# Newton steps of six mLSTM heads' normalization on GpSimd in place of VectorE

## The chip, the cores and the metric

The kernel runs on one NeuronCore of one Trainium2 chip. A core has a matrix engine (TensorE, PE in the profile, with PEld for its weight loads), a vector engine (VectorE, DVE), a scalar engine (ScalarE, ACT), GpSimd (POOL) and a queue that only issues DMAs (SyncE, SP). Each engine takes its own queue in order; semaphores order the engines against each other. The metric is the device time of one execution in microseconds (us).

## The reference

Two layers work on a sequence of 512 tokens of width 1024. The first is dilated window attention with a SwiGLU; the second, which the change touches, is an mLSTM mixer with eight heads and a SwiGLU. A final RMS norm follows. The end of the mLSTM mixer, cut to what matters:

```python
h = num / jnp.maximum(jnp.abs(den), jnp.exp(-m_t))[..., None]      # per head and token, 128 wide
...
h = h * lax.rsqrt(jnp.mean(h * h, axis=-1, keepdims=True) + RMS_EPS)
h = h.reshape(B, S, D_MODEL).astype(xn.dtype) * head_gain.astype(xn.dtype)
return (h * jax.nn.sigmoid(o_pre)) @ w_out
```

So each of the 8 heads needs one reciprocal square root per token: 512 numbers, which the kernel holds as 128 partitions by 4.

## The kernel before

All matrix products run on TensorE in a split form (a high and a low part of each operand, three products in place of one), 128 rows at a time, with 512 tokens as the free dimension. Weights come in chunks by SP's DMAs; ScalarE makes the high part of a chunk (line 209) and VectorE the low part (line 210, names ending in `_l`).

In the mLSTM stage the projections run as a stream of such products: `mqk` (queries and keys), `mv` (values, line 272), `mo` (output gate), then `mwo` (output product, line 240). The heads are threaded through that stream. For head h the function `decay` makes the exponent mask, `scores` the masked products (`m{h}s`, lines 1541 and 1542, weighted on VectorE in line 1543 into `m{h}e`), and `numerators` the rest: the numerators and denominators `m{h}num` on TensorE (line 1553), in two PSUM banks under the tag `o`, of which there are two; so the next head's numerators need the banks back. Then, on VectorE unless said otherwise:

- the denominators are copied to `rr` (line 1561), their absolute value and the lower bound taken (`aa`, 1562 and 1563), and inverted (1564);
- ScalarE squares the four blocks of the numerators, scaled by `rr`, and sums them into `s2` (line 1567); VectorE makes the mean and adds epsilon (1569);
- `rsqrt_newton` (lines 184 to 195) computes 1/sqrt of `s2`: an integer guess `y` in two operations (189, 190) and three Newton steps of three operations each (192, 193, 194), all on 128x4 elements;
- `rr` is multiplied by it (1571), and four operations scale the numerators out of PSUM into `yt` (1574), which frees the banks, the first with the second operation;
- for heads 0 to 5 a transpose in 32x32 blocks follows (`yB`, 1581), four DMAs to DRAM and one back (`yD`, `y`, lines 1584 and 1587), all issued by GpSimd. Heads 6 and 7 (`LAST_OUTPUTS`) are transposed on TensorE instead (`outputs`, `m6yT`, `m7yT`).

The result `y[h]` is multiplied by the gate later (line 1621). `rsqrt_newton` also serves the RMS norms (`inverse_rms`).

The program gives the work in one order, with `defer` and `at_tick` placing the heads' functions in the stream of projections. A planner of the language then writes each engine's queue, by its own estimate of when each instruction can start; so a change of one instruction's engine can move others on all queues. Beside its DMAs GpSimd copies `ql` (line 1512) and clears buffers in this stage. Near the kernel's end it scales the final gain (line 1659) and multiplies by it (1684).

Of the kernel before, what the change touches and what calls it, by code (L numbers as in the profile page):

```python
# [15 lines left out]
ALU = mybir.AluOpType  # L16
# [6 lines left out]
TB = SEQ // P  # L23
# [16 lines left out]
LAST_OUTPUTS = {6: 22, 7: 23}  # L40
# [31 lines left out]
def tile_hybrid_dilated_attn_mlstm(  # L72
# [4 lines left out]
    nc = tc.nc  # L77
# [3 lines left out]
    def pool(stack, name, **kw):  # L81
        return stack.enter_context(tc.tile_pool(name=name, bufs=1, **kw))
# [98 lines left out]
    def acc_tile(name):  # L181
        return ps.tile([P, 512], F32, tag="acc", name=name, bufs=3)

    def rsqrt_newton(tp_pool, v, n, name, y=None):

        if y is None:
            y = tp_pool.tile([P, n], F32, tag="rs_y%d" % n, name=name + "_y", bufs=2)
        a = tp_pool.tile([P, n], F32, tag="rs_a%d" % n, name=name + "_a", bufs=2)
        nc.vector.tensor_single_scalar(a.bitcast(I32), v.bitcast(I32), 1, op=ALU.arith_shift_right)
        nc.vector.tensor_scalar(y.bitcast(I32), a.bitcast(I32), -1, 0x5F3759DF, op0=ALU.mult, op1=ALU.add)  # L190
        for _ in range(3):
            nc.vector.scalar_tensor_tensor(a, y, -0.5, y, op0=ALU.mult, op1=ALU.mult)
            nc.vector.tensor_tensor(a, a, v, op=ALU.mult)
            nc.vector.scalar_tensor_tensor(y, a, 1.5, y, op0=ALU.add, op1=ALU.mult)
        return y
# [112 lines left out]
    def inverse_rms(v, name, box=None, then=None):  # L308
# [5 lines left out]
        def finish():  # L314
            nc.vector.tensor_scalar(v, v, 1.0 / D, EPS, op0=ALU.mult, op1=ALU.add)
            rsqrt_newton(npl, v, TB, name + "r", r)
            rhl = npl.tile([P, 2, TB], F32R, tag="rhl", name=name + "rhl", bufs=2)
            nc.vector.tensor_copy(rhl[:, 0], r)
            nc.vector.tensor_tensor(rhl[:, 1], r, rhl[:, 0].bitcast(F32), op=ALU.subtract)
            for part in range(2):  # L320
                dg = parts[part] = npl.tile([P, SEQ], F32R, tag=("ssum", "sq")[part], name=name + "dg",
                                               bufs=1 + part)
                for tb in range(TB):
                    nc.vector.tensor_scalar(dg[:, tb * P:(tb + 1) * P], ident,
                                            rhl[:, part, tb:tb + 1].bitcast(F32), None, op0=ALU.mult)
# [20 lines left out]
    with ExitStack() as actx:  # L346
# [16 lines left out]
        ang, n, sn, cs = (tmp[:, 0, i * P:(i + 1) * P] for i in range(4))  # L363
# [132 lines left out]
        v = npl.tile([P, TB], F32, tag="rs_v4", name="xv", bufs=2)  # L496
# [781 lines left out]
    with ExitStack() as fctx:  # L1278
# [34 lines left out]
        def copy_half(t):  # L1313
            for m in range(4):
                nc.scalar.activation(F[1][m][:, ts[t]], F[0][m][:, ts[t]], AF.Copy)

        def add_sum(n):
            for m in range(4):
                o = old[4 * n + m][:, ts[1]]
                nc.vector.tensor_tensor(o, F[1][m][:, ts[0]], o, op=ALU.add)  # L1320

        def first_tiles():
            for m in range(4):
                natural(m, F[0][m])
        last = work(product, plain, {("P1", 3): lambda: copy_half(0), ("P5", 3): lambda: copy_half(1),
                                     ("P6", 3): lambda: add_sum(0), ("P7", 3): lambda: add_sum(1),
                                     ("P3", 3): first_tiles})
# [8 lines left out]
    with ExitStack() as mctx:  # L1336
        mp = pool(mctx, "mlstm")
# [6 lines left out]
        def y_tile(k, name):  # L1344
            return mp.tile([P, SEQ], F32, tag="my%d" % k, name=name)
# [94 lines left out]
        for b in range(TB):  # L1440
            ve.scalar_tensor_tensor(fblk[32 * b:32 * b + H], blk(lf)[:, b], bias2[:, 1:2], blk(t0)[:, b],
                                    op0=ALU.add, op1=ALU.add)
# [72 lines left out]
        y = [None] * H  # L1515
# [29 lines left out]
        def numerators(hh):  # L1545
            nm = "m%d" % hh
            sm = sms[hh]
            num = [ps.tile([P, 512], F32, tag="o", name=nm + "num", bufs=2) for _ in range(2)]
            nv = lambda qb: num[qb // 2][:, (qb % 2) * 256:(qb % 2) * 256 + P + 1]
            for qb in range(TB):  # L1550
                for kb in range(qb + 1):
                    o = (qb - kb) * P
                    nc.tensor.matmul(nv(qb), sm[kb][:, o:o + P], vaug[:, kb, hh, :],
                                     start=(kb == 0), stop=(kb == qb))

            rr = mp.tile([P, TB], F32, tag="rr", name=nm + "rr", bufs=2)
            aa = mp.tile([P, TB], F32, tag="aa", name=nm + "aa", bufs=2)
            s2 = mp.tile([P, TB], F32, tag="s2", name=nm + "s2", bufs=2)
            for t in range(2):
                den = num[t].rearrange("p (a b) -> p a b", a=2)[:, :, P]  # L1560
                nc.vector.tensor_copy(rr[:, 2 * t:2 * t + 2], den)
            nc.vector.scalar_tensor_tensor(aa, rr, -1.0, rr, op0=ALU.mult, op1=ALU.max)
            nc.vector.tensor_tensor(aa, aa, bcol[:, npair:, hh], op=ALU.max)
            nc.vector.reciprocal(rr, aa)
            for qb in range(TB):
                junk = mp.tile([P, P], F32, tag="junk", name=nm + "j", bufs=2)
                nc.scalar.activation(junk, nv(qb)[:, :P], AF.Square, scale=rr[:, qb:qb + 1],
                                     accum_out=s2[:, qb:qb + 1])
            nc.vector.tensor_scalar(s2, s2, 1.0 / P, EPS, op0=ALU.mult, op1=ALU.add)
            rq = rsqrt_newton(mp, s2, TB, nm + "rq")  # L1570
            nc.vector.tensor_tensor(rr, rr, rq, op=ALU.mult)
            yt = mp.tile([P, SEQ], F32, tag="yt", name=nm + "yt", bufs=2)
            for qb in range(TB):
                nc.vector.tensor_scalar(yt[:, qb * P:(qb + 1) * P], nv(qb)[:, :P], rr[:, qb:qb + 1], None,
                                        op0=ALU.mult)
            if hh in LAST_OUTPUTS:
                yts[hh] = yt
                return

            turned = npl.tile([P, SEQ], F32, tag="sq", name=nm + "yB", bufs=2)  # L1580
            nc.vector.transpose(turned.rearrange("p (c i) -> p c i", i=R), yt.rearrange("p (c i) -> p c i", i=R))
            d = mdp.tile([P, SEQ], F32, tag="yD", name=nm + "yD", bufs=3)
            for a in range(TB):
                nc.gpsimd.dma_start(d.rearrange("(f j) (q a i) -> a j q f i", f=4, q=TB, a=4)[a],
                                    turned[R * a:R * (a + 1)].rearrange("p (q f i) -> p q f i", q=TB, f=4))
            y[hh] = y_tile(hh, "y%d" % hh)
            nc.gpsimd.dma_start(y[hh], d)

        def outputs(hh):
            tp = ps.tile([P, 512], F32, tag="t", name="m%dyT" % hh, bufs=1)  # L1590
            for qb in range(TB):
                transpose_into(tp, qb, yts[hh][:, qb * P:(qb + 1) * P])
            y[hh] = y_tile(hh, "y%d" % hh)
            nc.scalar.activation(y[hh], tp, AF.Copy)
# [6 lines left out]
        for hh, ts in enumerate(HEAD_AT):  # L1601
            for t, fn in zip(ts, (decay, scores, numerators)):
                at_tick(t, lambda hh=hh, fn=fn: fn(hh))
# [26 lines left out]
    with ExitStack() as fctx:  # L1630
# [60 lines left out]
        def copy_banks(to, src):  # L1691
            for m in range(2):
                nc.scalar.activation(to[m], src[m], AF.Copy)

        def add_banks(tbs, src):
            for m, tb in enumerate(tbs):
                nc.vector.tensor_tensor(ht[tb, 1], src[m], ht[tb, 1], op=ALU.add)
# [12 lines left out]
        def plain(n, pi, a, w):  # L1710
            for t in range(2):
                multiply_half(((c11, u_), (p5, c22))[n][t], a, t, w)

        last = work(product, plain, {("P1", 3): lambda: copy_banks(u_, c11), ("P5", 3): lambda: copy_banks(c22, p5),
                                     ("P6", 3): lambda: add_banks((0, 1), u_), ("P7", 3): lambda: add_banks((2, 3), u_),
                                     ("P4", 0): lambda: outputs((0, 1), p5), ("P4", 1): lambda: outputs((2, 3), c22)})
# [6 lines left out]
        for acc, tb, cs in tiles:  # L1723
# [10 lines left out]
            else:  # L1734

                v, r, a2 = fv[:, tb:tb + 1], fr[:, tb:tb + 1], fa[:, tb:tb + 1]
                nc.vector.scalar_tensor_tensor(v, fss[:, tb, 2:3], 1.0 / D, fpre[:, tb:tb + 1],
                                               op0=ALU.mult, op1=ALU.add)
# [33 lines left out]
```

## Time and profile before

| | us |
|---|---|
| median of three runs (1409.32 to 1410.51) | 1409.42 |
| the profiled execution | 1409.1 |
| its span in the profile | 1407.0 |
| TensorE busy in it | 1395.9 |
| VectorE busy | 1045.6 |
| ScalarE busy | 659.5 |
| GpSimd busy | 145.4 |

The profile page has six parts: busy times; the span in 40 slices; DMA queues; the chain of work that ended last; the costliest groups of instructions; DMA issues. Other views are asked of the trace: groups by tile or line (duration as least, median and greatest in ns, first and last start in us), who waited for whom (total us, times, longest), instructions in order of time (start, length, engine, line, operation, output and inputs, then the idle time ahead of it and what ended it), and busy time by windows. In a window's row stand the window, its length, then busy us and count of PE, PEld, DVE, ACT and POOL, then TensorE's granted clock, the DMA share and GB/s. The mLSTM stage's heads 0 to 7 lie between 920 and 1025 us. TensorE's busy time is modelled from pipelined instructions.

### The profile page before, as it was taken

The page shows a single profiled execution, that of the slowest core. Times are in us where ns is not written, and L with a number is a line of the kernel's source. Part 1 is how long each engine was busy: PE and PEld are TensorE (multiplying, and loading weights), DVE is VectorE, ACT ScalarE, POOL GpSimd, SP SyncE. Part 2 cuts the span into 40 slices and gives each one's busy share as a digit, 9 for nine tenths or more (in the row PEclk, how much of TensorE's full clock was granted, in tenths as well). Part 3 has the DMA queues.
Part 4 walks back from the last instruction along what each step waited for, and adds up shares of the span by engine and source line. Part 5 has one row for each costly group of instructions (what it writes and reads, how often), then busy time and mean ns, then how long its engine had stood idle before and what let it go on. Part 6 is the DMA issues. An engine that isn't in the chain of part 4 may idle for free.

```text
span 1407.0 us, 21031 instructions
## 1 busy us (share of the span) xinstructions
PE 1395.9 (99%) x8154; PEld 1235.5 (88%) x8154; DVE 1045.6 (74%) x1816; ACT 659.5 (47%) x1096; POOL 145.4 (10%) x216
## 2 busy tenths in 40 slices
PE   9999999999999999999999999999999999999998
PEld 7888888888888888999999998888888899999886
DVE  7866557566567298777877788998758888887785
ACT  5333224224225153444576354786534444458744
POOL 1011011002002000000010101113101230002111
PEclk9999999999999999999999999999999999999999
DMA  6346245334434444333264543234333553335871
GB/s 194 98 113 201 77 117 154 125 105 129 163 102 120 160 118 152 91 120 118 67 186 97 150 120 84 85 90 103 96 101 105 168 151 116 120 99 141 173 188 61
DMA packets 136381, 174.44 MB, mean 124 GB/s; under 512 B 8469, under 2 KB 111189, under 8 KB 136281
## 3 DMA queue, kind: packets, MB, share of 16 engines
q1 hardware_dynamic: 121088, 133.65, 30.3%
q0 software_dynamic: 13536, 38.33, 12.3%
q8 instruction: 64, 1.05, 0.3%
q10 hardware_dynamic: 1656, 1.12, 0.2%
q14 instruction: 37, 0.30, 0.1%
HBM read 157.34 MB, written 15.73 MB: 123 GB/s over the span
## 4 chain that ended last, share of the span: by engine, by line
PE 92%; DVE 5%; ACT 2%; issue 1%; ACTq 0%; DVEq 0%
PE fo L1292 8%; PE f0j_u L1017 5%; PE f1j_u L1017 5%; PE f1j L240 5%; PE f0j L240 5%; PE f1j_p L1017 3%; PE f0j_p L1017 3%; PE f1j_c L1017 3%; PE f0j_c L1017 3%; PE mwo L240 3%; PE awo L240 3%; PE mo L240 3%; PE finu L1674 2%; PE finc L1674 2%; PE finp L1674 2%; PE a3g12v L298 2%
## 5 line engine op out<-in xcount | busy, mean ns | idle before, releaser
L240 PE MATMUL f0j<-n_h,f0j_h 128*128 128x512 f32 x96 | 37.5, 390 | 0.0
L240 PE MATMUL f1j<-n_h,f1j_h 128*128 128x512 f32 x96 | 37.5, 390 | 0.0
L240 PE MATMUL f1j<-n_h,f1j_l 128*128 128x512 f32 x96 | 37.4, 389 | 0.0
L240 PE MATMUL f0j<-n_h,f0j_l 128*128 128x512 f32 x96 | 37.4, 389 | 0.0
L240 PE MATMUL f0j<-n_l,f0j_h 128*128 128x512 f32 x96 | 37.3, 389 | 0.0
L240 PE MATMUL f1j<-n_l,f1j_h 128*128 128x512 f32 x96 | 37.3, 389 | 0.0
L1135 POOL DMA_DIRECT2D f0S<-in_ffn_w_out_dram x7 | 6.5, 1019 | 265.6 <-ACT f0P L1114 146.6
L1644 POOL DMA_DIRECT2D hD<-hB x32 | 20.7, 653 | 96.3 <-DVE hB L1641 96.3
L539 DVE TENSOR_TENSOR rot<-rot,sinr 32x1024 f32<-32x1024 f32 x24 | 28.9, 1205 | 0.0
L240 PE MATMUL mo<-n_h,mo_k_h 128*128 128x512 f32 x64 | 25.3, 395 | 0.0
L240 PE MATMUL mo<-n_h,mo_k_l 128*128 128x512 f32 x64 | 25.2, 394 | 0.0
L240 PE MATMUL mo<-n_l,mo_k_h 128*128 128x512 f32 x64 | 25.1, 393 | 0.0
L240 PE MATMUL mqk<-n_h,mqk_k_h 128*128 128x512 f32 x64 | 25.1, 393 | 0.0
L240 PE MATMUL mwo<-yo_l,mwo_k_h 128*128 128x512 f32 x64 | 25.1, 393 | 0.0
L240 PE MATMUL mqk<-n_l,mqk_k_h 128*128 128x512 f32 x64 | 25.1, 392 | 0.0
L240 PE MATMUL awo<-ao_h,awo_k_h 128*128 128x512 f32 x64 | 25.1, 392 | 0.0
L240 PE MATMUL mwo<-yo_h,mwo_k_l 128*128 128x512 f32 x64 | 25.0, 391 | 0.0
L240 PE MATMUL mqk<-n_h,mqk_k_l 128*128 128x512 f32 x64 | 25.0, 390 | 0.0
L240 PE MATMUL awo<-ao_h,awo_k_l 128*128 128x512 f32 x64 | 25.0, 390 | 0.0
L240 PE MATMUL awo<-ao_l,awo_k_h 128*128 128x512 f32 x64 | 24.9, 390 | 0.0
L240 PE MATMUL mwo<-yo_h,mwo_k_h 128*128 128x512 f32 x64 | 24.9, 391 | 0.0
L240 PEld LDWEIGHTS f0j<-n_h,f0j_l 128*128 128x128 f32 x96 | 18.0, 188 | 3.8
(2271 smaller groups left out, 5427.9 us busy)
## 6 DMA issues: line engine op xcount, KB each, us to landing
f0j_w<-in_ffn_w_in_dram SPq DMA_DIRECT2D x28, 512.0 KB, 4.4
f1j_w<-in_ffn_w_in_dram SPq DMA_DIRECT2D x28, 512.0 KB, 4.1
f1T<-in_ffn_w_out_dram POOLq DMA_DIRECT2D x12, 512.0 KB, 7.0
awo_k_w<-in_attn_w_out_dram SPq DMA_DIRECT2D x8, 512.0 KB, 5.8
mv_k_w<-in_mlstm_w_in_dram SPq DMA_DIRECT2D x8, 512.0 KB, 3.7
mqk_k_w<-in_mlstm_w_in_dram SPq DMA_DIRECT2D x8, 512.0 KB, 3.8
mo_k_w<-in_mlstm_w_in_dram SPq DMA_DIRECT2D x8, 512.0 KB, 3.7
mwo_k_w<-in_mlstm_w_out_dram SPq DMA_DIRECT2D x8, 512.0 KB, 3.5
```

The costliest lines, as they stand in the source:

```text
L240: nc.tensor.matmul(acc, whl[a][:, k, m * P:(m + 1) * P], pairs[b][kk], start=(kk == 0 and (a, b) == SPLITS[0]), stop=(kk == nk - 1 and (a, ...
L298: nc.tensor.matmul(accs[tb], pairs[a][kk][:, tb * P:(tb + 1) * P], whl[b][:, k, :], start=(kk == 0 and (a, b) == SPLITS[0]), stop=(kk == K ...
L539: nc.vector.tensor_tensor(sh, sh, sinr.unsqueeze(1).to_broadcast([R, 2, SEQ]), op=ALU.mult)
L1017: nc.tensor.matmul(acc[name][:, m * HALF:(m + 1) * HALF], whl[a][:, k, m * P:(m + 1) * P], ops[okey][b][:, k], start=(fresh and m == 0 and ...
L1135: nc.gpsimd.dma_start(t, src[1][:, ks], accum_op=ALU.add)
L1292: nc.tensor.matmul(acc, w[a_][:, k, m * P:(m + 1) * P], b[b_][k], start=(fresh and k == 0 and (a_, b_) == SPLITS[0]), stop=(k == 1 and (a_ ...
L1644: nc.gpsimd.dma_start(hD[k // 4].rearrange("(b i) x -> i b x", i=R)[:, :, c0:c0 + R], t[R * a_:R * (a_ + 1)])
L1674: nc.tensor.matmul(acc[m], a[a_][k][:, (2 * t + m) * P:(2 * t + m + 1) * P], w[b_][:, k, :], start=(fresh and k == 0 and (a_, b_) == SPLIT ...
```

## The change

For heads 0 to 5 the three Newton steps and the product into `rr` are put on GpSimd. A step there has four operations in place of three, since the fused scalar-tensor-tensor form is written out as products and a scalar operation. The guess, the mean and the scaling stay on VectorE; heads 6 and 7 and the RMS norms stay as they were.

```diff
-    def rsqrt_newton(tp_pool, v, n, name, y=None):
+    def rsqrt_newton(tp_pool, v, n, name, y=None, on_gpsimd=False):
...
         for _ in range(3):
+            if on_gpsimd:
+                nc.gpsimd.tensor_tensor(a, y, y, op=ALU.mult)
+                nc.gpsimd.tensor_tensor(a, a, v, op=ALU.mult)
+                nc.gpsimd.tensor_scalar(a, a, -0.5, 1.5, op0=ALU.mult, op1=ALU.add)
+                nc.gpsimd.tensor_tensor(y, a, y, op=ALU.mult)
+                continue
             nc.vector.scalar_tensor_tensor(a, y, -0.5, y, op0=ALU.mult, op1=ALU.mult)
             nc.vector.tensor_tensor(a, a, v, op=ALU.mult)
             nc.vector.scalar_tensor_tensor(y, a, 1.5, y, op0=ALU.add, op1=ALU.mult)
...
-            rq = rsqrt_newton(mp, s2, TB, nm + "rq")
-            nc.vector.tensor_tensor(rr, rr, rq, op=ALU.mult)
+
+            last = hh in LAST_OUTPUTS
+            rq = rsqrt_newton(mp, s2, TB, nm + "rq", on_gpsimd=not last)
+            (nc.vector if last else nc.gpsimd).tensor_tensor(rr, rr, rq, op=ALU.mult)
```

In the built program the queues of TensorE, VectorE, ScalarE and GpSimd stand in another order between the first head and the last; SP's queue has the same order. On GpSimd a configuration step that stood ahead of line 1659 stands ahead of head 0's first Newton step.

## The prediction

> **What bounds the kernel now.** I read the page's busy shares first, then who waited for whom on TensorE, then the mLSTM stretch by windows and by tiles.
>
> ```profile
> span 1407.0 us, 21031 instructions
> PE 1395.9 (99%) x8154; PEld 1235.5 (88%) x8154; DVE 1045.6 (74%) x1816; ACT 659.5 (47%) x1096; POOL 145.4 (10%) x216
> ```
> ```profile
> PE m2num L1553 <- DVE m1yt L1574: 1.2, 1, 1.2
> ```
> ```profile
> 940.00:950.00 10.00, 10.00 (x85) 9.95 (x84) 9.66 (x27) 9.82 (x21) 1.40 (x3) 1.00 0.46 134
> 950.00:960.00 10.00, 8.76 (x59) 7.64 (x59) 8.67 (x27) 8.06 (x26) 3.56 (x5) 1.00 0.34 79
> ```
>
> TensorE (PE) is the bound: 1395.9 of 1407.0 us. In the stretch with the heads it loses 1.2 us to one wait, m2's numerators for m1's scaling (the window 950 to 960 shows the gap: 8.76 of 10). So the change can give back some 1.2 us, 0.1%. VectorE (DVE) is nearly full there (9.66 of 10), but PE does not wait for it. What the change can cost is decided by the chain of one head.
>
> ```profile
> L1553 PE MATMUL m0num<-vaug,m0e x20: 272/275/275, 921.6 to 923.7; 128*128 128x129 f32 x20
> L1553 PE MATMUL m1num<-vaug,m1e x20: 271/275/275, 933.9 to 936.1; 128*128 128x129 f32 x20
> L1553 PE MATMUL m2num<-vaug,m2e x20: 275/275/349, 952.0 to 954.2; 128*128 128x129 f32 x20
> L1553 PE MATMUL m3num<-vaug,m3e x20: 275/275/348, 963.6 to 965.8; 128*128 128x129 f32 x20
> L1553 PE MATMUL m4num<-vaug,m4e x20: 275/275/348, 975.1 to 977.3; 128*128 128x129 f32 x20
> L1553 PE MATMUL m5num<-vaug,m5e x20: 272/275/275, 986.9 to 989.0; 128*128 128x129 f32 x20
> L1553 PE MATMUL m6num<-vaug,m6e x20: 275/275/348, 997.3 to 999.5; 128*128 128x129 f32 x20
> ```
> ```profile
> L1574 DVE TENSOR_SCALAR m2yt<-m2num,m2rr x4: 343/343/352, 962.8 to 963.6; 128x128 f32<-128x128 f32 x4
> L1574 DVE TENSOR_SCALAR m4yt<-m4num,m4rr x4: 341/341/351, 986.1 to 986.9; 128x128 f32<-128x128 f32 x4
> ```
>
> Numerators of head h+1 need the first of the two PSUM banks that head h's scaling (yt) frees with its second operation. m2's yt begins at 962.8, its second operation ends some 0.7 us later, at 963.5, and m3num begins at 963.6; m4's yt begins at 986.1, and m5num at 986.9. PE stays busy until that moment because other matmuls are queued ahead of m3num in just that amount. PE takes its queue in order: whatever lengthens the way from num(h) to yt(h) beyond the matmuls queued between num(h) and num(h+1) stops PE. I call those matmuls the cover.
>
> **The change part by part.** Six heads lose ten DVE operations each (nine Newton steps and the product into rr) and gain thirteen on GpSimd (POOL), each waiting for the one before. The guess stays on DVE.
>
> *DVE's gain.*
> ```profile
> L194 DVE SCALAR_TENSOR_TENSOR m1rq_y<-m1rq_a,m1rq_y x3: 157/162/565, 944.6 to 949.7; 128x4 f32<-128x4 f32 x3
> L190 DVE TENSOR_SCALAR m0rq_y<-m0rq_a x1: 170/170/170, 928.9 to 928.9; 128x4 int32<-128x4 int32 x1
> L190 DVE TENSOR_SCALAR m1rq_y<-m1rq_a x1: 166/166/166, 942.7 to 942.7; 128x4 int32<-128x4 int32 x1
> L190 DVE TENSOR_SCALAR m2rq_y<-m2rq_a x1: 170/170/170, 958.4 to 958.4; 128x4 int32<-128x4 int32 x1
> L190 DVE TENSOR_SCALAR m3rq_y<-m3rq_a x1: 160/160/160, 969.7 to 969.7; 128x4 int32<-128x4 int32 x1
> L190 DVE TENSOR_SCALAR m4rq_y<-m4rq_a x1: 170/170/170, 980.7 to 980.7; 128x4 int32<-128x4 int32 x1
> L190 DVE TENSOR_SCALAR m5rq_y<-m5rq_a x1: 160/160/160, 992.6 to 992.6; 128x4 int32<-128x4 int32 x1
> ```
> 60 operations of about 0.16 us are 9.6 us of DVE. They lie beside a busy PE and are worth only the 1.2 us above.
>
> *One POOL step.* No row has a 128x4 arithmetic step on POOL; the nearest are these.
> ```profile
> L1684 POOL TENSOR_TENSOR ht<-ht,gbc 128x512 f32<-128x512 f32 x3 | 3.9, 1290 | 43.6 <-ACT fsq L1682 43.6
> L1684 POOL TENSOR_TENSOR ht<-ht,gbc 128x256 f32<-128x256 f32 x2 | 1.6, 806 | 1.7 <-ACT fsq L1682 1.7
> L389 POOL COPY sinn<-angles 32x128 f32<-32x128 f32 x4 | 1.1, 285 | 7.4 <-DVE angles L384 7.3
> L1352 POOL MEMSET pre<- 128x3 f32 x2 | 0.1, 95 | 50.2 <-PE fo L1292 50.2
> ```
> ```profile
> 1393.59 0.18 ACT L1682 ACTIVATION_READ_ACCUMULATOR fsq<-ht 128x1 f32 x1
> 1393.81 0.16 DVE L1737 SCALAR_TENSOR_TENSOR fv<-fss,fpre 128x1 f32<-128x1 f32 x1 [0.79 <-ACT fsq L1682]
> 1393.86 1.29 POOL L1684 TENSOR_TENSOR ht<-ht,gbc 128x512 f32<-128x512 f32 x1 [3.09 <-ACT fsq L1682]
> ```
> The line through the two products is 1.9 ns an element and 0.32 us at none; the memset of three elements takes 0.095, so 0.1 to 0.32. ACT ends at 1393.77; DVE starts 0.04 us later, POOL 0.09. With that handover a step is 0.14 (a memset and 0.04) at the least. At the most I take 0.6, the 0.32 and three such handovers. I take 0.30 (0.2 and 0.1), nearer to the small rows because four elements are nearest to three. Thirteen steps: 3.9 us (1.8 to 7.8).
>
> *The chain against its cover.* From num to the end of the guess, before: m0 921.6 to 929.1, 7.5; m1 8.9; m2 6.6; m3 6.3; m4 5.8; m5 5.9. The built order of the changed kernel puts more DVE work ahead of three guesses: for m2 some splits of ql and score products (estimate 1.4 net of DVE's idle time), for m4 a weight split and two 512-wide operations among the denominators (2.2), for m5 the like (1.6). So 7.5, 8.9, 8.0, 6.3, 8.0, 7.5. Add 3.9, and 0.8 for rr to the second yt: 12.2, 13.6, 12.7, 11.0, 12.7, 12.2.
>
> The cover follows from before's gaps between num starts (12.3, 18.1 of which 1.4 idle or stretched, 11.6, 11.5, 11.8, 10.4) and from what the order moves:
> ```profile
> 969.32 0.39 PE L240 MATMUL mo<-n_h,mo_k_h 128*128 128x512 f32 x1
> 971.84 0.40 PE L240 MATMUL mo<-n_h,mo_k_l 128*128 128x512 f32 x1
> 941.92 0.28 PE L272 MATMUL mv<-mv_k_h,n_l 128*128 128x256 f32 x1
> 944.44 0.28 PE L272 MATMUL mv<-mv_k_h,n_l 128*128 128x256 f32 x1
> ```
> Eleven steps of mo take 2.52 us, 0.23 each; 21 of mv 2.52, 0.12 each. m1num moves behind 12 mqk and 3 score matmuls (2.75 + 0.65), m2num ahead of 22 mv (2.65), m3num ahead of 3 scores and 2 mo, m4num ahead of 10 mo less the 3 scores, m5num ahead of 5 mo, m6num behind 15. Covers: 15.7, 10.7, 13.0, 9.9, 10.65, 13.8. Short of cover: m1 by 2.9, m3 by 1.1, m4 by 2.05; sum 6.0 us. m0, m2, m5 have 3.5, 0.3 and 1.6 left.
>
> *Sharing with DVE.*
> ```profile
> 906.94 1.23 DVE L210 TENSOR_TENSOR mqk_k_l<-mqk_k_w,mqk_k_h 128x1024 fp32r<-128x1024 f32 x1
> 906.98 1.67 POOL L1512 CAST ql<-ql 64x512 fp32r<-64x512 f32 x1 [0.60 <-DVE ql L1511]
> 951.39 0.61 POOL L1512 CAST ql<-ql 64x512 fp32r<-64x512 f32 x1 [4.09 <-DVE ql L1511]
> ```
> A cast takes 0.61 us alone and 1.67 when a DVE subtraction of two SBUF tensors began 0.04 before it; the 565 ns among m1rq_y's 162 fall in a POOL cast too. So a chain of short POOL steps loses time to each long two-input DVE operation placed between guess and yt: m1 has one (a conv step, 0.75), m2 two ks splits and a weight split (2.65), m3 a weight split (1.23), m4 none. Estimate: 0.6, 1.2 after m2's spare, 1.0: 2.8 us. If POOL gets in between, 0.
>
> *The queues.*
> ```profile
> 954.18 2.94 POOL L1584 DMA_DIRECT2D m1yD<-m1yB  x4 [2.17 <-DVE m2rr L1561]
> 960.93 0.56 POOL L1587 DMA_DIRECT2D y<-m1yD  x1 [3.81 <-DMA m1yD<-m1yB]
> ```
> POOL takes its queue in order, and m1's four DMA issues (2.94 us) now stand ahead of m2's chain, m0's ahead of m1's, and so on. In before they begin 2.9 us after m1yt (951.3) and end at 957.1, 5.1 us after m2num; m2's guess ends at 958.6, and comes later still after the change. So the issues are done in time; if they were late, all of POOL's chain behind them would be. The wait for m1yD to land (3.81 us, to 960.9) now stands within m2's chain, after eight steps, 2.4 us behind a guess at 8.0 us after num, 962.4 on before's clock: free by 1.5 us. In the other heads the landing is waited for after rr. SP's order is unchanged. The last of the six outputs, y5, passes through such DMAs before DVE reads it; for that I keep 0 to 2 us in the range.
>
> Sum: 6.0 + 2.8 - 1.2 = 7.6 us. The profiled execution took 1409.1, so 1416.7; the median is 1409.4, so I say 1417.0.
>
> *Code on POOL.* The built program puts a configuration step before the first arithmetic step.
> ```profile
> 1278.42 0.54 POOL L1658 DMA_DIRECT2D gbc<-in_final_norm_dram  x1 [126.23 <-ACT f1j20S_h L209]
> 1283.56 3.82 POOL L1659 TENSOR_SCALAR gbc<-gbc 128x1024 f32<-128x1024 f32 x1 [4.60 <-DMA gbc<-in_final_norm_dram]
> 926.98 1.07 POOL L1512 CAST ql<-ql 64x512 fp32r<-64x512 f32 x1 [18.34 <-DVE m0rr L1564]
> ```
> In before it stands between these two, where 4.60 us are waited for a DMA anyway; now it stands behind the cast that ends at 928.05, and m0's guess ends at 929.1. A load of 4.6 us would end at 932.65: 3.55 late, m0's spare is 3.5, so I count nothing. If the 3.82 were load too (8.4 in all) it costs 3.9. The Trainium skill, GPSIMD Engine Reference, section 2.1, states a load of about 6 us at the first call to freshly loaded code; by it the estimate is 1.4 us more, 1418.4. No row here shows the load by itself.
>
> **The rivals.** Slow steps: 0.6 us each, from the rows above. Short of cover: 0.4, 6.8, 3.6, 5.0, 6.0, 2.3, 24.1 in all; with sharing and the gain, 1435. For it: 0.32 us is what the products' line gives. Against: the copy of 128 elements takes 0.285 whole.
>
> The other side, quick steps: the sum falls under 2.8 us when a step is below 0.16 us with sharing, or below 0.25 without; m1's shortfall is then 1 to 2 us and m3's and m4's nearly nothing. At 0.14 it is 0.8 - 1.2, so 1409.0. For it: the memset's 0.095. Against: the copy of 128 elements takes 0.285, and the cast of 1.67 shows sharing.
>
> The load not hidden: 1421 at 3.9 us more.
>
> **How the numbers follow.** Forecast (steps of 0.2 to 0.45): 0.55. Slow steps: 0.13. Load: 0.08. Quick steps, no change: 0.2. Over 0.2% faster: 0.04, since only 1.2 us (0.09%) is there to win; it would need a gain no row shows. 0.2% (2.8 us) is about what a measurement of this kernel can tell from no change. Slower sums to 0.76. The range runs from 1410 (quick steps' edge) to 1428 (steps near 0.5).
>
> **What would show it.** After: POOL steps of 128x4 spaced by 0.3 us; waits of PE m2num, m3num, m4num and m5num for yt of the head before, about 3.5, 1, 2 and 2 us; DVE idle before yt for POOL's rr; the loss all between 920 and 1030. Wrong would be: PE waits under 2 us there (steps quicker, no sharing), a gap before m1num (load), or a loss elsewhere.

## The result, and the profile after

The changed kernel takes 1421.09 us (median of 6 executions, 1418.78 to 1421.54) against 1409.21 us for the kernel before (6 executions): a ratio of 1.0083, with a 95% interval of 1.0072 to 1.0094. It is 11.9 us slower; the forecast was 1417.0, within 1410 to 1428. Lines of the code stand 6 to 8 further down than before: numerators 1559, `yt` 1582, `rr`'s product 1579, the Newton steps 193 to 196.

The head of the page of the changed kernel, in the profiled execution (1421.54 us):

```profile
span 1419.8 us, 21049 instructions
PE 1400.5 (99%) x8154; PEld 1240.4 (87%) x8154; DVE 1039.8 (73%) x1756; ACT 659.7 (46%) x1096; POOL 164.6 (12%) x294
```

The span grew by 12.8 us, and TensorE's busy time by 4.6 of them although it runs the same 8154 matmuls. So there are two losses: TensorE stands still for longer, and it is also slower while it works. The waits first, by who waited for whom, between 900 and 1040 us (total, times, longest):

```profile
PE m3num L1559 <- DVE m2yt L1582: 3.4, 1, 3.4
PE m2num L1559 <- DVE m1yt L1582: 2.4, 1, 2.4
PE m5num L1559 <- DVE m4yt L1582: 1.5, 1, 1.5
PE m1num L1559 <- DVE m0yt L1582: 0.9, 1, 0.9
PE m7s L1547 <- DVE m7e L1549: 0.9, 1, 0.9
PE m1nb L1527 <- ACT m0e L1537: 0.4, 1, 0.4
PE m4num L1559 <- DVE m3yt L1582: 0.3, 1, 0.3
```

They sum to 9.8 us. In the kernel before, the same view gives 1.2 (m2num), 0.4 (m1nb) and 0.2: 1.8. So 8.0 us are new waits, and five of the seven are numerators that wait for the scaling of the head before. The same view of VectorE shows what that scaling waited for:

```profile
DVE m2yt L1582 <- POOL m2rr L1579: 3.3, 1, 3.3
DVE m1yt L1582 <- POOL m1rr L1579: 2.6, 1, 2.6
...
DVE m4yt L1582 <- POOL m4rr L1579: 1.5, 1, 1.5
```

With 1.5 for m5, 1.2 for m3 and 0.6 for m0 VectorE stands 10.7 us for GpSimd's `rr`. The other 4.8 us are the clock. Busy time by windows, cut where the granted clock changes (window, length, then PE, PEld, DVE, ACT, POOL, then the clock):

```profile
948.56:951.98 3.42, 1.01 (x9) 0.83 (x8) 1.11 (x5) 2.65 (x4) 2.22 (x10) 1.00 0.28 100
951.98:955.39 3.41, 3.41 (x18) 3.41 (x18) 2.74 (x6) 2.68 (x5) 1.81 (x3) 0.50 0.43 101
955.39:958.80 3.41, 3.41 (x30) 3.41 (x30) 2.92 (x6) 2.14 (x8) 3.05 (x4) 1.00 0.39 58
...
965.63:969.04 3.41, 0.65 (x3) 0.19 (x2) 0.14 (x2) 0.00 (x0) 2.32 (x10) 1.00 0.67 171
969.04:972.46 3.42, 2.82 (x13) 2.82 (x14) 1.94 (x6) 0.00 (x0) 1.31 (x2) 0.50 0.16 60
972.46:975.87 3.41, 3.41 (x14) 3.04 (x14) 0.66 (x4) 2.35 (x10) 1.65 (x3) 0.50 0.50 77
```

The clock changes only at the edges of stretches of 3.41 us. Where TensorE was busy for 1.01 or 0.65 us of one, the next ran at 0.50. Work at half the clock costs half its time: 3.41 / 2 = 1.7 us in the first place, (2.82 + 3.41) / 2 = 3.1 us in the second, together 4.8. Waits and clock give 8.0 + 4.8 = 12.8 us, the whole difference of the spans; counted the other way, TensorE is busy for 4.6 us more and idle for 8.2 us more. In before the clock is 1.00 in every window of this stage.

### The profile page after: what moved, and what is told of

It is laid out like the page before. It is cut to its first block, busy times and chain, and to the rows that moved or that the text cites. A ratio compares the mean times of both kernels' runs of the same rounds, so it can differ in the third digit from the quotient of the medians.

```text
span 1419.8 us, 21049 instructions
## 1 busy us (share of the span) xinstructions
PE 1400.5 (99%) x8154; PEld 1240.4 (87%) x8154; DVE 1039.8 (73%) x1756; ACT 659.7 (46%) x1096; POOL 164.6 (12%) x294
## 3 DMA queue, kind: packets, MB, share of 16 engines
q0 software_dynamic: 13536, 38.33, 12.2%
## 4 chain that ended last, share of the span: by engine, by line
PE 88%; DVE 5%; ACT 3%; POOL 2%; issue 2%; ACTq 0%; DVEq 0%; POOLq 0%
PE fo L1298 8%; PE f1j_u L1023 5%; PE f0j_u L1023 5%; PE f0j L246 5%; PE f1j L246 5%; PE f1j_p L1023 3%; PE f0j_p L1023 3%; PE f1j_c L1023 3%; PE f0j_c L1023 3%; PE awo L246 3%; PE mwo L246 3%; PE finu L1682 2%; PE finc L1682 2%; PE finp L1682 2%; PE a3g12v L304 2%
## 5 line engine op out<-in xcount | busy, mean ns | idle before, releaser
L1652 POOL DMA_DIRECT2D hD<-hB x32 | 20.6, 650 | 99.3 <-DVE hB L1649 99.3
L246 PEld LDWEIGHTS f1j<-n_h,f1j_l 128*128 128x128 f32 x96 | 18.0, 188 | 3.8
```

Source lines behind the costliest of these rows:

```text
L246: nc.tensor.matmul(acc, whl[a][:, k, m * P:(m + 1) * P], pairs[b][kk], start=(kk == 0 and (a, b) == SPLITS[0]), stop=(kk == nk - 1 and (a, ...
L1652: nc.gpsimd.dma_start(hD[k // 4].rearrange("(b i) x -> i b x", i=R)[:, :, c0:c0 + R], t[R * a_:R * (a_ + 1)])
```

## The experiments

All times are medians; the kernel before ran beside each set (1408.99 in the first, 1409.02 in the second, 1408.90 in the third).

| kernel | us | over before | ratio, 95% interval |
|---|---|---|---|
| changed | 1421.09 | +11.9 | 1.0083 (1.0072 to 1.0094) |
| changed, again | 1421.25 | +12.4 | 1.0087 (1.0073 to 1.0100) |
| head 4 alone | 1408.66 | -0.3 | 1.0000 (0.9991 to 1.0009) |
| head 4 alone, 16 more steps | 1408.92 | -0.1 | 1.0001 (0.9991 to 1.0010) |
| head 2 alone | 1409.45 | +0.4 | 1.0003 (0.9994 to 1.0012) |
| heads 3, 4, 5 | 1412.85 | +3.8 | 1.0028 (1.0016 to 1.0039) |
| heads 0, 1, 2 | 1416.67 | +7.7 | 1.0055 (1.0040 to 1.0070) |
| two steps in place of three | 1412.44 | +3.4 | 1.0025 (1.0016 to 1.0035) |
| four operations, on VectorE | 1410.73 | +1.7 | 1.0014 (1.0005 to 1.0024) |
| copies of ql on ScalarE | 1420.56 | +11.7 | 1.0084 (1.0071 to 1.0098) |
| copy out of PSUM | 1416.90 | +7.9 | 1.0063 (1.0048 to 1.0078) |
| copy out of PSUM, scaling held back | 1412.08 | +3.2 | 1.0022 (1.0011 to 1.0032) |
| before, with the copy out of PSUM | 1407.69 | -1.2 | 0.9993 (0.9984 to 1.0001) |

The theory at the start: GpSimd's chain is longer than the matmuls queued in its cover, so TensorE waits for a PSUM bank, and a long wait halves the clock. The rivals: waits alone; the count of operations, not their engine; something else of GpSimd (its queue, its sharing with VectorE, VectorE's own standing).

### The engine or the count of operations

In the changed kernel, for the same six heads:

```diff
-                nc.gpsimd.tensor_tensor(a, y, y, op=ALU.mult)
-                nc.gpsimd.tensor_tensor(a, a, v, op=ALU.mult)
-                nc.gpsimd.tensor_scalar(a, a, -0.5, 1.5, op0=ALU.mult, op1=ALU.add)
-                nc.gpsimd.tensor_tensor(y, a, y, op=ALU.mult)
+                nc.vector.tensor_tensor(a, y, y, op=ALU.mult)
+                nc.vector.tensor_tensor(a, a, v, op=ALU.mult)
+                nc.vector.tensor_scalar(a, a, -0.5, 1.5, op0=ALU.mult, op1=ALU.add)
+                nc.vector.tensor_tensor(y, a, y, op=ALU.mult)
...
-            (nc.vector if last else nc.gpsimd).tensor_tensor(rr, rr, rq, op=ALU.mult)
+            nc.vector.tensor_tensor(rr, rr, rq, op=ALU.mult)
```

> The kernel before with the Newton step in the change's four operations in place of three, for the same six heads, but all on VectorE. It tells the count of operations from the engine. Three more operations of 0.16 us a head make the chain 0.5 us longer: by the theory of chain against cover TensorE's wait grows by 0 to 0.5 us a head, 0 to 1.5 us over the kernel before in all, and the clock stays 1.0. If the count of steps rather than their engine made the loss, most of the 12 us would be here.

It is 1.7 us over before, a little above the 0 to 1.5 expected. TensorE's waits:

```profile
PE m2num L1559 <- DVE m1yt L1582: 2.0, 1, 2.0
PE m7yT L312 <- DVE m7yt L1582: 0.5, 1, 0.5
```

m2num waits 2.0 in place of 1.2 us: a longer chain without cover shows even on VectorE. But the count explains some 1.7 of 12 us, and the engine, together with the order that the planner builds for it, the rest. No run changes the engine and holds the order of the queues.

### One head alone

```diff
-            last = hh in LAST_OUTPUTS
+            last = hh != 4
```

> Only head 4 has its Newton steps on GpSimd; the other five keep them on VectorE as before the change. In the changed kernel m5's numerators waited 1.5 us for m4's scaling, and no halved clock followed that wait. Both theories (waits alone; waits and then a halved clock) expect here one wait of 1 to 2 us at m5num, a clock of 1.0 throughout the stretch, and 1 to 2 us over the kernel before (1.000 to 1.0015 of it). If the loss came from VectorE standing idle rather than from TensorE's wait, nothing would be lost, since VectorE has idle time around head 4 in the kernel before.

Nothing was lost, and no numerators waited for m4's scaling: a miss for both theories as I had put them. The planner had changed TensorE's order. One of the three products of `mo` between m4's and m5's numerators, in the kernel with head 4 alone, by lines within that stretch:

```profile
L246 PE MATMUL mo<-n_h,mo_k_h 128*128 128x512 f32 x21 | 8.4, 398 | 0.0
```

and in the changed kernel with six heads:

```profile
L246 PE MATMUL mo<-n_h,mo_k_h 128*128 128x512 f32 x10 | 4.1, 406 | 0.0
```

Twice as many matmuls stand in the cover of a lone long head. They are drawn ahead from later products, and the heads after it, short again, don't miss them. The next run made the lone chain much longer:

```diff
-            last = hh in LAST_OUTPUTS
+            last = hh != 4
...
+            if not last:
+                for _ in range(16):
+                    nc.gpsimd.tensor_scalar(rq, rq, 1.0, 0.0, op0=ALU.mult, op1=ALU.add)
```

> As the kernel with head 4 alone on GpSimd, with sixteen more dependent GpSimd steps on 128x4 in that head (times 1, plus 0: the values stay). At 0.28 us a step and an estimated 0.165 us that the planner allows for one (the 1.5 us wait of m4's thirteen steps in the changed kernel), m5's numerators should wait 1.8 us longer, 3.3 us or so; up to 6 us if the planner puts no cover in. Theory with the clock: a wait over 2.4 us is followed by a halved TensorE clock of 3.4 or 6.8 us, worth 1.7 to 3.4 us more, so 5 to 9 us over the kernel before. Theory of waits alone: clock 1.0 after the wait, the time longer by the wait alone, 3.3 to 6 us, and the halved clock of the changed kernel had another cause.

A second miss, by the same cause: counted from the start of m4's numerators, m4's `yt` came after 20.6 us in place of 14.3, and m5's numerators were put off with it, from 18.6 to 21.3 us, with TensorE busy all the time. 29 dependent steps on GpSimd cost nothing where there is work to draw ahead.

### Does the loss belong to a head or to the row?

```diff
-            last = hh in LAST_OUTPUTS
+            last = hh != 2
```

> Only head 2 has its Newton steps on GpSimd: the head after which TensorE waited longest (3.4 us) in the changed kernel. Theory of each head against its own cover (the prediction's): m3's numerators wait 2 to 3.4 us and, if 2.3 us of it fall into one of the 3.41 us stretches in which the clock is set, the clock halves once: 2 to 7 us over the kernel before. Theory of a shared stock (the planner draws later projections ahead of the numerators after a long head, and only a row of long heads uses them up): 55 instead of 24 matmuls of mo now stand between m2's and m3's numerators, no wait of m3num over 0.3 us, the time within 1 us of the kernel before, as with head 4 alone.

Within 0.5 us of before, no wait of m3num: for a lone head the shared stock was right, and covers carried over from the kernel with six long heads were wrong. Head 1, after which TensorE waits for 1.2 us even in before, was not run alone. Then two halves:

```diff
-            last = hh in LAST_OUTPUTS
+            last = hh not in (3, 4, 5)
```

> Heads 3, 4 and 5 on GpSimd, heads 0, 1 and 2 as before the change. In the changed kernel the waits after these heads were 0.3 (m4num), 1.5 (m5num) and none, with the clock whole: 0 to 1.8 us over the kernel before if losses belong to heads. If loss comes with the length of the row of long heads, half of six would lose some 3 to 6 us. By the shared stock, 64 matmuls of mo stand after m3's numerators, 28 and 31 after m4's and m5's: a wait at m5num or m6num of 1 to 2.5 us at most, none at m4num, clock 1.0.

```profile
PE m6num L1559 <- DVE m5yt L1582: 2.2, 1, 2.2
...
PE m5num L1559 <- DVE m4yt L1582: 0.8, 1, 0.8
```

```diff
-            last = hh in LAST_OUTPUTS
+            last = hh not in (0, 1, 2)
```

> Heads 0, 1 and 2 on GpSimd, heads 3, 4 and 5 as before the change. TensorE's order up to m3's numerators is that of the changed kernel. If the losses belong to this part of the stage (no output projections can be drawn ahead there yet), m1num, m2num and m3num wait about 0.9, 2.4 and 3.4 us again and the clock halves after the longer ones: 7 to 11 us over the kernel before (the clock's part is 0 to 4.8, since it hangs on where the wait falls in the fixed stretches of 3.41 us). If loss goes with the number of long heads alone, it is half of 12 us, spread over the three.

```profile
PE m3num L1559 <- DVE m2yt L1582: 3.3, 1, 3.3
PE m2num L1559 <- DVE m1yt L1582: 2.4, 1, 2.4
PE m1num L1559 <- DVE m0yt L1582: 0.9, 1, 0.9
```

Both rows show the same pattern: the first head costs least (0 and 0.9 us) and each later one more (0, 0.8, 2.2 and 0.9, 2.4, 3.3). With heads 0 to 2, the waits and the clock's three halved stretches are those of the changed kernel; the profiled execution was the slowest of four (1415.32 to 1418.46), so its clock stands for the upper end. With heads 3 to 5 it was the quickest of seven (1411.81 to 1414.38), with a whole clock; what the slower ones lost is not seen. The halves cost 3.8 and 7.7 us, 11.5 together, about the whole, but that they add up is partly chance: alone, heads 3 to 5 bring waits of 0.8 and 2.2 us at m5num and m6num, in the changed kernel 1.5 and none. So long heads in a row cost, and most in the first three.

### A shorter chain

The third Newton step is left out for the six heads.

```diff
-        for _ in range(3):
+        for _ in range(2 if on_gpsimd else 3):
```

> The changed kernel with two Newton steps in place of three for the six heads (the third step is left out, so the last digits of the normalization are left out too). Each chain is four GpSimd steps shorter, 1.1 us at 0.28 us. Taking 1.1 us from each wait of the changed kernel leaves 0, 1.3, 2.3, 0 and 0.4 us at m1num to m5num, 4.0 in all, 2.8 over the kernel before; with the clock rule (a halved clock only after 2.3 us idle or more within one fixed stretch) 0 to 3.4 more. So 1412 to 1415. If the chain's length is not what counts, the time stays at 1420.

```profile
PE m2num L1559 <- DVE m1yt L1582: 2.0, 1, 2.0
PE m3num L1559 <- DVE m2yt L1582: 1.5, 1, 1.5
PE m4s L1547 <- DVE m4e L1549: 1.2, 1, 1.2
PE m5num L1559 <- DVE m4yt L1582: 0.6, 1, 0.6
```

1412.44 us, within the expected 1412 to 1415. Four of thirteen steps fewer a head take 8.5 of 11.9 us away. The waits, with m1nb's 0.4, sum to 5.7 us in place of 9.8, and no stretch is idle for long enough to halve the clock, which is 1.00 in the whole stage: 4.1 and 4.8 us less than in the changed kernel's profile. The loss is not proportional to the length of the chain.

### The copy of ql in GpSimd's queue

In the changed kernel a copy stood between two Newton steps of m0 (in order of time: start, length, engine, line, operation):

```profile
931.67 0.20 POOL L194 TENSOR_TENSOR m0rq_a<-m0rq_a,m0s 128x4 f32<-128x4 f32 x1
935.66 0.83 POOL L1518 CAST ql<-ql 64x512 fp32r<-64x512 f32 x1 [3.79 <-DVE ql L1517]
936.58 0.51 POOL L195 TENSOR_SCALAR m0rq_a<-m0rq_a 128x4 f32<-128x4 f32 x1
```

```diff
-                nc.gpsimd.tensor_copy(ql[oth], ql[own].bitcast(F32))
+                nc.scalar.activation(ql[oth], ql[own].bitcast(F32), AF.Copy)
```

> The changed kernel with the copies of ql on ScalarE instead of GpSimd. The copy that stood between two of m0's Newton steps held that chain for 4.4 us (3.79 of it waiting for VectorE). If that queue step is why m1's numerators waited 0.9 us, m0's thirteen steps now run through in 3.7 to 4.5 us and m1num's wait is gone, 1 to 2 us less than the changed kernel if the planner keeps the rest, 1418 to 1420; the waits after heads 1 and 2 stay at 2 to 3.5 us each, since their chains hold no such copy. If ScalarE's queue suffers from the copies, exponentials come late and the gain is lost.

m0's thirteen steps ran through in 3.55 us (930.08 to 933.63), yet m1num still waited 1.1 us, now with its numerators put 4 us earlier (934.3 for 938.3) by the planner, and the time hardly moved. Without the copy the planner gives m0 a cover of 10.7 us in place of 15.9, so this run does not isolate the copy. The changed kernel's own trace says more: there m0's chain took 16.7 us from its numerators to the second operation of `yt`, and the copy held it for 4.4 of them; 12.3 would have lain 3.6 us within the cover of 15.9. In that order of the queues the copy accounts for m1num's 0.9 us; taking it away brought another order, and no gain. The first step also shows no visible cost of loading GpSimd's code:

```profile
930.08 0.20 POOL L193 TENSOR_TENSOR m0rq_a<-m0rq_y 128x4 f32<-128x4 f32 x1 [82.03 <-DVE m0rq_y L190]
```

It begins 0.08 us after VectorE's guess ended (930.00), GpSimd having been idle for 82 us; a load within that time would not show.

### Is it the PSUM bank?

In the changed kernel the numerators are copied to SBUF at once, and squared and scaled there, so the banks come free before the Newton steps.

```diff
+            yt = mp.tile([P, SEQ], F32, tag="yt", name=nm + "yt", bufs=2)
+            for t in range(2):
+                nc.vector.tensor_copy(yt[:, 2 * t * P:2 * (t + 1) * P].rearrange("p (a b) -> p a b", a=2),
+                                      num[t].rearrange("p (a b) -> p a b", a=2)[:, :, :P])
+            nv = lambda qb: yt[:, qb * P:(qb + 1) * P]
...
-            yt = mp.tile([P, SEQ], F32, tag="yt", name=nm + "yt", bufs=2)
```

> The changed kernel, but VectorE copies each head's numerators out of PSUM right after the denominators and scales them in place in SBUF, so that the PSUM banks are free before the Newton steps begin. If the loss is the numerators waiting for a PSUM bank and what follows from that wait, the waits at m1num to m5num for the scaling go, the clock stays at 1.0, and the time comes to within 2.8 us of the kernel before (1408 to 1412), although GpSimd's steps stay as they are. If GpSimd's chain costs by another way (its ports shared with VectorE, VectorE's idle time, the output's DMAs), the time stays near 1418 to 1421. The two copies of 256 elements a row per head are about 1 us more VectorE work each head.

The waits at the numerators went, but the time fell by 4.2 us only, to 1416.90, between the two expectations, and the clock, expected whole, was halved once. So the bank is not the whole cause. TensorE's longest waits in this kernel:

```profile
PE m6s L1547 <- DVE m6e L1549: 3.1, 1, 3.1
PE m3s L1547 <- DVE m3e L1549: 2.5, 1, 2.5
PE m4s L1547 <- DVE m4e L1549: 1.3, 1, 1.3
```

What m6e stood behind is seen in VectorE's order of time:

```profile
986.40 0.87 DVE L1586 TENSOR_SCALAR m4yt<-m4yt,m4rr 128x128 f32<-128x128 f32 x4 [3.66 <-POOL m4rr L1584]
...
989.85 0.69 DVE L1549 SCALAR_TENSOR_TENSOR m6e<-m6s,m6e 128x512 f32<-128x512 f32 x1
```

VectorE takes its queue in order. It stood 3.66 us at m4's scaling for GpSimd, and m6's masked scores, which did not need m4 at all, were queued behind it; TensorE waited for them. Over the six heads it stood 12.9 us. The control is the kernel before with the same copy, the diff above applied to it:

> The kernel before with the same copy out of PSUM and nothing on GpSimd: the control for the kernel with the copy. If the copy itself, 1 us of VectorE work a head, costs by filling VectorE up in the stretch where it is 97% busy, it shows here: 2 to 5 us over the kernel before. If the 8 us of that kernel come from GpSimd's chain and not from the copy, this one lies within 1.5 us of the kernel before (1407.8 to 1410.5), TensorE's 1.2 us wait at m2num gone.

1407.69 us, m2num's 1.2 us gone: the copy costs nothing. It is the quickest kernel here, but its interval reaches 1.0001, so a gain is not shown. GpSimd's chain thus costs 9.2 us (1416.90 less 1407.69, from two sets) with the banks free; the four executions behind 1416.90 lie between 1416.06 and 1421.01. To test VectorE's standing, each head's scaling and transposition, and with them its output's DMAs, are held back until the next head's guess has been issued:

```diff
+            def finish():
                 for qb in range(TB):
...
+            pending.append(finish)
+            if hh in LAST_OUTPUTS:
+                while pending:
+                    pending.pop(0)()
+            elif len(pending) > 1:
+                with tc.issue_after(last_on(mybir.EngineType.DVE)):
+                    pending.pop(0)()
```

> The kernel with the copy out of PSUM, and the scaling and the transposition of head h held back on VectorE until head h+1's guess has been issued, so that GpSimd's steps of head h have the whole of head h+1's front to run in. With the copy alone VectorE stood 12.9 us for GpSimd's rr, and TensorE then waited 8.3 us for the masked scores that VectorE had behind it. If VectorE's standing in its queue is what was left of the loss, those waits fall under 1 us each and the time comes back to 1408 to 1411, with all thirteen GpSimd steps a head still there. If GpSimd's steps cost by themselves (ports, DMAs, the clock), it stays at 1414 to 1418.

VectorE's waits for `rr` fell from 12.9 to 1.5 us and the time by 4.8 us, to 1412.08: just above the expected 1411. Of the masked scores' waits, expected under 1 us each, three stayed above it. The 4.4 us that are left over the control have a place in the trace too, though no run tests it. TensorE's waits:

```profile
PE m7s L1547 <- DVE m7e L1549: 2.2, 1, 2.2
PE m4s L1547 <- DVE m4e L1549: 1.3, 1, 1.3
PE m3s L1547 <- DVE m3e L1549: 1.3, 1, 1.3
```

m4s waits 1.3 us in the control as well. m7e stood behind a VectorE operation that waited 2.43 us for a DMA of m3's output. The four DMAs before it had landed by 989.6, but GpSimd issued it only after ten of m5's Newton steps:

```profile
991.56 0.62 POOL L194 TENSOR_TENSOR m5rq_a<-m5rq_a,m5s 128x4 f32<-128x4 f32 x1
992.14 0.60 POOL L1602 DMA_DIRECT2D y<-m3yD  x1
```

```profile
995.15 0.69 DVE L1644 SCALAR_TENSOR_TENSOR y<-og,y 128x512 f32<-128x512 f32 x1 [2.43 <-DMA y<-m3yD]
```

And the clock was halved once after TensorE's wait at m7s. m3s goes back to GpSimd's queue as well. m3e stood on VectorE behind m0's scaling, which waited 1.48 us for `rr`, and m0's chain had stood on GpSimd behind the first step of m1, put between two of m0's steps, which waited 4.24 us for m1's guess (the kernel with the copy alone has the same, 4.27 us):

```profile
937.20 0.42 POOL L193 TENSOR_TENSOR m1rq_a<-m1rq_y 128x4 f32<-128x4 f32 x1 [4.24 <-DVE m1rq_y L190]
```

```profile
939.82 0.88 DVE L1589 TENSOR_SCALAR m0yt<-m0yt,m0rr 128x128 f32<-128x128 f32 x4 [1.48 <-POOL m0rr L1586]
```

m7s 2.2, m3s 1.3 and about 1.6 for the clock make 5.1, against 4.8 between the profiled spans (1410.7 and 1405.9).

### Waits alone, or waits and the clock

The changed kernel once more, unaltered.

> The changed kernel unaltered, executed more times, to part the waits from the clock: TensorE's order and waits are the same in each execution, while the fixed stretches of 3.41 us in which the clock is set begin at another moment of each. If the halved clock adds its own part, the executions spread by 1.7 us for each halved stretch: those with the highest mean clock near 1418 (waits alone: 8.2 us over the kernel before), those with three halved stretches near 1421.5. If the waits are all, the times do not go with the mean clock and stay within 1 us of each other.

Times and mean clocks go together: 1421.79 and 1421.63 at 0.995, 1420.88 at 0.996, 1419.19 at 0.998. In the first set it was 1421.54, 1421.48 and 1421.27 at 0.995, 1420.56 at 0.996, 1420.91 at 0.997 and 1418.78 at 0.998, so only the pair at 0.996 and 0.997 is out of order, by 0.35 us. The same program spreads by 2.6 and 2.8 us with the clock granted, so waits alone are not the whole; they would give 1409.2 + 8.0 = 1417.2, and the quickest of the ten executions took 1418.78. The kernel before has a mean of 0.998 in its profile too, with no halved stretch in the stage, since the clock is also halved behind the last matmul (from 1402.48 us on); so 0.998 does not tell whether the quickest executions had a halved stretch. What idle time is enough can be read across kernels. In the kernel with the scaling held back, a stretch and the one that followed:

```profile
992.70:996.11 3.41, 1.50 (x8) 0.91 (x6) 0.98 (x3) 0.00 (x0) 3.34 (x8) 1.00 0.55 125
996.11:999.52 3.41, 3.16 (x9) 2.58 (x10) 3.35 (x9) 0.00 (x0) 0.08 (x1) 0.50 0.19 29
```

and with the copies on ScalarE:

```profile
956.98:960.39 3.41, 1.52 (x7) 0.95 (x6) 3.30 (x7) 3.40 (x15) 0.00 (x0) 1.00 0.05 18
960.39:963.80 3.41, 1.14 (x6) 0.91 (x6) 1.29 (x4) 3.40 (x11) 2.16 (x12) 1.00 0.53 154
963.80:967.22 3.42, 2.25 (x10) 2.25 (x11) 2.63 (x9) 1.81 (x3) 0.94 (x3) 0.50 0.00 0
```

TensorE busy 1.50 us of the 3.41 or less: the next stretch is halved. Busy 1.52 or more: it isn't (with heads 3 to 5 the least was 1.57, and the clock stayed whole). The 2.3 us of idle time that I had taken for the limit before were too many; 1.9 are enough. A run that fills the waits with spare matmuls, to keep the clock up with the waits unchanged, was not made; the clock's price rests on these windows and on the spread of one program.

## Why the prediction was right, and where it was not

The direction, the place and the mechanism (a longer chain against the matmuls in its cover) were right, and 1421 lies in the range of 1410 to 1428. The value is 4 us short, and a term that the sum does not have, TensorE's clock, accounts for it. That the waits came out at nearly the forecast total is in part luck, since their errors by head cancel.

**What bounds the kernel.** Right: TensorE, and the way from num(h) through the chain to yt(h), in the stretch 920 to 1010 us. Of before's 1.2 us at m2num nothing was recovered; that wait became 2.4. VectorE's busy time fell by 5.8 us and not by 9.6.

**One POOL step.** Right. 0.30 us was taken; the steps of an undisturbed head are 0.28 apart, thirteen of them 3.54 us (990.54 to 994.08) where 3.9 was reckoned:

```profile
990.54 0.19 POOL L193 TENSOR_TENSOR m4rq_a<-m4rq_y 128x4 f32<-128x4 f32 x1 [2.73 <-DVE m4rq_y L190]
990.81 0.20 POOL L194 TENSOR_TENSOR m4rq_a<-m4rq_a,m4s 128x4 f32<-128x4 f32 x1
...
993.88 0.20 POOL L1579 TENSOR_TENSOR m4rr<-m4rr,m4rq_y 128x4 f32<-128x4 f32 x1
```

**Sharing with DVE.** Right in kind. The steps that fell beside VectorE's large two-input operations were longer; the two below began within weight splits that VectorE began at 964.48 (1.23 us) and 979.25 (1.21 us):

```profile
964.61 1.16 POOL L193 TENSOR_TENSOR m2rq_a<-m2rq_y 128x4 f32<-128x4 f32 x1
...
979.45 1.06 POOL L195 TENSOR_SCALAR m3rq_a<-m3rq_a 128x4 f32<-128x4 f32 x1
```

Beyond 0.20 us each the steps took 0.3 us in m0, 0.35 in m1, 1.7 in m2, 0.9 in m3 and 0.9 in m5. In m1, m2 and m3, for which 2.8 was reckoned, that makes 3.0; m5's 0.9 cost no wait, since m6num waited for nothing.

**The chain against its cover.** The sum was right, the places were not. Short of cover and sharing, less 1.2, made 7.6 us; 8.0 were measured. But m1num was put at nothing and took 0.9, m2num was put at 3.5 us and took 2.4, m3num 1 and took 3.4, m4num 2 and took 0.3, m5num 2 and took 1.5, and 0.9 came at m7s, which the sum does not have.

The covers, read from the built order, were right. TensorE's busy time from one head's numerators to the next, with the halved clock's part taken off, was 15.9, 10.9, 12.9, 9.9, 10.4 and 14.0 us for m0 to m5; the forecast had 15.7, 10.7, 13.0, 9.9, 10.65 and 13.8. So the step that failed is the length of single chains. From num to the second `yt`, m0 took 16.7 us (12.2 forecast), m1 13.1 (14.2 with the sharing), m2 18.0 (14.2), m3 13.2 (12.0), m4 11.7 (12.7). m0's excess is the copy in GpSimd's queue, 4.4 us. m2's has three parts: its numerators ran at half clock (4.1 us for 2.5), its guess came 1.3 us later than that alone explains, with VectorE waiting 1.1 us for m4's scores, and the issue of m1's last DMA stood in GpSimd's queue after eight of its steps, which lengthened the chain by 0.9 us:

```profile
966.99 0.60 POOL L1595 DMA_DIRECT2D y<-m1yD  x1 [0.38 <-issue]
```

The slow numerators by themselves do not explain m3num's wait, because the halved clock stretched m2's cover by 1.7 us as well as the chain by 1.6. For m4num it did help: the halved clock stretched m3's cover by 3.1 us, up to 975.87, and its numerators by 2.2 only. Besides, the chains of m1 and m4, and m3's without the clock's part, were about 1 us shorter than reckoned, so m2num, m5num and m4num waited less.

**The numerators' bank as the only way.** Incomplete. With the banks free, GpSimd's steps still cost 7.9 us over the kernel before and 9.2 over the control. Holding the scaling back took 4.8 of them away, so VectorE, standing in order for `rr`, accounts for about half by experiment; the trace places the rest. The prediction looked for VectorE's idle time before yt but counted nothing for what was queued behind it.

**The queues.** Counted as free, which is wrong: a copy of `ql` that waited 3.79 us stood in GpSimd's queue within m0's chain, and the prediction did not look for it. It used up the 3.5 us that m0 had to spare, and m1num waited 0.9. The DMA issue among m2's steps was foreseen, and it waited for no landing, but its own 0.9 us were not counted.

**Code on POOL.** Right, as far as it shows: at most 1.19 us lie between the copy before and m0's first step, and 0.08 us between guess and step where GpSimd was idle before. The load of about 6 us of the Trainium skill (GPSIMD Engine Reference, section 2.1) is not visible in any run here; a load under idle time would not be.

**The sum.** Here the miss of 4 us lies: waits were counted once, and nothing for TensorE's clock after them, 4.8 us in the profiled execution. The forecast wait of 3.5 us, and those of 2 if they fall within one stretch, were themselves long enough for it. The Trainium skill, TensorE: Matmul & The Clock Gate, Part 1, tells of free-running windows of 3413 ns; the trace agrees, with stretches of 3.41 us whose edges lie elsewhere in each execution. The same page of the Trainium skill, section HAM oscillation, warns of idle gaps over about 3.4 us; here 1.9 us idle within one stretch were enough, so the measurement decides.

**The rivals.** Slow steps (0.6 us) and quick ones (0.14) are both refuted by 0.28. The load's 1421 came out as a number, for another reason.

## What to carry to other kernels

When a short chain moves to another engine, count the wait of whoever reads its result, and then everything queued in order behind that reader; freeing a buffer helps only as far as no queue stands still. The engine that takes the chain over has a queue too, and what the planner puts between the steps lengthens the chain. A long chain cost nothing alone (heads 2 and 4 here), where later matmuls could be drawn into its cover, and cost when several stood in a row. A TensorE wait near 2 us should be priced with the halved stretch that can follow it: two such waits here cost 4.8 us beside their own 5.8.

## What the hardware showed that I had not expected

In these traces TensorE's clock goes in stretches of 3.41 us by how busy the one before was: after 1.50 us busy or less at full clock the next was halved, and from 1.52 on it wasn't. A halved stretch that was itself busy for 2.25 or 2.82 us was followed by another halved one; after 3.16 or 3.41 the clock came back. The edges of the stretches fall elsewhere in each execution (951.98 and 951.52 us in the two profiles of the changed kernel), so what a wait costs depends on how it falls on them, and it was nothing, 1.7 or 3.1 us more: with the copy out of PSUM a wait of 2.5 us lay across two stretches (busy 1.58 and 2.72 us) and the clock stayed whole, one of 3.1 us fell mostly into one (busy 1.13) and halved the next.
